# Latent attention by pairs of heads: 64-row score tiles and values stored split

## The chip, the cores and the metric

The kernel runs on one core of one Trainium2 chip. The metric is the device time of one execution in microseconds (us); the time of a kernel is the median of several executions. A core has five engines that run side by side, each with its own queue of instructions in a fixed order: TensorE (PE, matrix products; PEld is its loading of weights), VectorE (DVE), ScalarE (ACT), GpSimd (POOL) and SyncE (SP), which here only issues transfers (DMA). They work on an on-chip memory of 128 partitions (SBUF). Matrix products go into a small second memory of eight banks (PSUM), from which VectorE and ScalarE fetch them.

## The reference

The model is a trunk of two layers over 1024 tokens of width 1024, all in 32-bit floats. Layer 0 is differential attention, layer 1 is latent attention; a gated MLP with a short causal convolution follows each. Only layer 1's attention changes:

```python
def mla_attention(h, w_in, q_norm_g, kv_norm_g, w_uq, w_ukv, w_o, cos, sin):
    proj = h @ w_in                                            # 384 + 256 + 32 columns
    c_q = rms_norm(proj[..., :384], q_norm_g)
    c_kv = rms_norm(proj[..., 384:640], kv_norm_g)
    k_pe = apply_rope(proj[..., 640:], cos, sin)               # one rotary key for all heads
    q = (c_q @ w_uq).reshape(b, s, 16, 64 + 32)
    q_nope, q_pe = q[..., :64], apply_rope(q[..., 64:], cos, sin)
    kv = (c_kv @ w_ukv).reshape(b, s, 16, 64 + 64)
    k_nope, v = kv[..., :64], kv[..., 64:]
    # for each block of 128 queries
    sc = (einsum(q_nope, k_nope) + einsum(q_pe, k_pe)) * 96 ** -0.5
    p = masked_softmax(sc, chunk_mask)                         # key chunk (64) <= query chunk
    return einsum(p, v).reshape(b, s, 1024) @ w_o
```

There are 16 heads. A head's query and key have 64 plain columns and 32 rotary ones; the 32 rotary columns of the key are shared by all heads.

## The kernel before

**Precision.** A 32-bit operand x is held as a high part (x rounded to a format that TensorE takes at full speed, `hi`, L124) and a low part (x minus the high part, `lo`, L130). A product is three matmuls: high x low, high x high, low x high (`mm3`, L117 to L122). So L120, L121 and L122 are the lines of nearly every product, and L128 and L131 those of nearly every split.

**Stages of layer 1.** `mla_input` (L1540) makes the latents, token block by token block, transposes them, and makes the values (`values`, L1603), which go to DRAM (`v_d`) as plain floats. `mla_heads` (L1674) then works on 16 heads. Its projections are "units" of one half (512 tokens) each, written as generators that issue their matmuls, yield, and then empty the accumulator:

- `q_unit` (L1708), one for each head and half: 3 products of 3 matmuls. The weights have 128 columns a head: 64 plain, 32 rotary and the same 32 with their halves swapped, so that the rotation is one multiply by a table (L1720), after which 128 rows stand in one tile: plain, cosine part, sine part. High and low part follow.
- `k_unit` (L1724), one for a pair of heads and half: 2 products of 3 matmuls, 128 columns for two heads. It is emptied in two 64-row pieces into the key tiles of the two heads.
- The rotary key is rotated once and copied into rows 64 to 127 of four key tiles (`rotary`, `share`).
- `fetch_v`, `split_v` load a pair's values from `v_d` and split them.

**Steps.** The attention of a head is four steps. Step p has query blocks 2p and 2p+1 (of 128 queries each); block i has (i+1) x 128 keys. `MlaStep.scores` (L2005) makes one block's scores with three matmuls of 128 rows for each 512 keys into one score buffer S, masks the corner (L2017), takes the negated row maximum (L2018), and the exponential with its sum (L2019). `weigh` takes the reciprocal (L2025) and scales the row on GpSimd (L150). `turn` (L255) transposes the probabilities into banks "b" (L264) and splits them; `product` (L2028) multiplies with the split values into bank "u" (L2039, L2040), and adds the two halves of the result (L2042, L2043).

There are two S buffers of two banks each, three banks "b", shared by units and transposes, and one bank "u". `steps` (L293) is the program order: scores of this step's first block, a unit, the transposes of the step before, scores of the second block, units, the product of the step before. A scheduler reorders this by its own estimate of times: what is ready and stands first in program order goes first; an engine's order is then fixed. (In layer 0's attention the order is written out by hand; its scores, L1884, are already pairs of 64-row matmuls.) The steps of a head come in the order 1, 0, 3, 2. Strings such as `QUERIES_LOW` choose the engine of each split.

## Time and profile before

| | |
|---|---|
| time, median of 3 | 2373.07 us (2372.19 to 2373.26) |
| profiled execution: time, span | 2372.74 us, 2370.9 us |
| granted TensorE clock | 0.999 |
| busy share of PE, DVE, ACT, POOL | 99%, 81%, 53%, 25% |
| attention of layer 1: first to last masking (L2017) | 1289.7 to 1627.0 us of the span |

The span goes from the first to the last instruction. In a timeline row stand start, duration, engine, line, operation, the tile written and the tiles read, and the shape; brackets give the idle time before it and what ended it. In a row of groups the count is followed by the busy time, the mean of one in ns, and the engine's idle time before them with what ended it. Matmuls are pipelined, so their durations overlap.

### The profile page before, as it was taken

Reading aid. Unit: us, or ns where it says so; the run is one execution under the profiler, and the core shown is the slowest. Engines: PE = TensorE matmul, PEld = TensorE weight load, DVE = VectorE, ACT = ScalarE, POOL = GpSimd, SP = SyncE. Lnnn points to the kernel's source line nnn. Section 1 sums busy time; section 2 is a strip of 40 time slices with the busy share of each in tenths; the row PEclk is TensorE's granted clock in tenths of the full one; section 3 lists DMA queues with packets and bytes.
Section 4 is the critical chain, followed back from the end, with each engine's and each line's share of the span. In section 5 each row is a group of like instructions: output and inputs, shape, how many; then the busy total and the mean of one; then the engine's idle time right before and its main releaser. Section 6 shows DMA issues by size and latency. Waiting matters only on the chain.

```text
span 2370.9 us, 32976 instructions
## 1 busy us (share of the span) xinstructions
PE 2345.3 (99%) x12146; PEld 1976.2 (83%) x12146; DVE 1919.9 (81%) x3170; ACT 1259.6 (53%) x2315; POOL 583.5 (25%) x465
## 2 busy tenths in 40 slices
PE   9999999999999999999999999999999999999998
PEld 7888888788888888888898889988888888888886
DVE  6777878858888888999865888886588888889997
ACT  5666666745444444354444777775454444443444
POOL 4545444323000000000133666673420000000001
PEclk9999999999999999999999999999999999999999
DMA  3111111332222222652221211133322222227502
GB/s 148 40 36 36 49 37 54 111 134 94 89 80 81 80 89 80 234 174 86 84 99 56 72 33 39 41 98 110 114 79 88 80 80 83 87 80 284 178 1 80
DMA packets 95667, 213.42 MB, mean 90 GB/s; under 512 B 8713, under 2 KB 33937, under 8 KB 95505
## 3 DMA queue, kind: packets, MB, share of 16 engines
q1 hardware_dynamic: 86304, 183.51, 23.5%
q10 hardware_dynamic: 9200, 27.80, 3.2%
q8 instruction: 96, 1.57, 0.3%
q14 instruction: 67, 0.54, 0.1%
HBM read 158.85 MB, written 52.43 MB: 89 GB/s over the span
## 4 chain that ended last, share of the span: by engine, by line
PE 91%; DVE 5%; DMA 1%; ACT 1%; issue 1%; POOL 0%; POOLq 0%; DVEq 0%; SPq 0%; ACTq 0%
PE S L122 14%; PE S L120 14%; PE S L121 14%; PE b L120 9%; PE b L122 8%; PE b L121 8%; PE u L120 5%; PE u L122 5%; PE u L121 4%; PE S L1884 3%; PE b L264 2%; PE u L2040 1%; PE b L1930 1%; PE u L2039 1%; DVE s L131 1%
## 5 line engine op out<-in xcount | busy, mean ns | idle before, releaser
L168 POOL TENSOR_TENSOR st<-st,mhalf 128x1 f32<-128x1 f32 x56 | 35.3, 632 | 1296.1 <-DVE st L165 1287.4
L120 PE MATMUL S<-s,u 128*128 128x512 f32 (+1 forms) x800 | 301.8, 377 | 0.2 <-ACT u L1110 0.2
L122 PE MATMUL S<-s,u 128*128 128x512 f32 (+1 forms) x800 | 301.2, 376 | 0.1
L121 PE MATMUL S<-s,u 128*128 128x512 f32 (+1 forms) x800 | 301.0, 376 | 0.0
L128 ACT CAST u<-h 128x512 fp32r<-128x512 f32 (+1 forms) x194 | 115.8, 619 | 267.1 <-DVE h L1031 262.8
L120 PE MATMUL b<-s,u 128*128 128x512 f32 x588 | 230.8, 393 | 1.1 <-DVE u L131 0.4
L122 PE MATMUL b<-s,u 128*128 128x512 f32 x588 | 229.1, 390 | 0.0
L121 PE MATMUL b<-s,u 128*128 128x512 f32 x588 | 229.0, 389 | 0.0
L1088 DVE SCALAR_TENSOR_TENSOR u<-u,conv,u 128x1023 f32<-128x1023 f32 (+1 forms) x176 | 225.1, 1279 | 0.8 <-ACT u L1084 0.7
L150 POOL TENSOR_TENSOR u<-u,st 128x512 f32<-128x512 f32 (+7 forms) x160 | 173.1, 1090 | 161.1 <-DVE st L2025 107.3
L128 ACT CAST s<-u 128x512 fp32r<-128x512 f32 (+3 forms) x229 | 144.2, 663 | 100.2 <-PE u L122 28.7
L128 ACT CAST u<-b 128x512 fp32r<-128x512 f32 (+1 forms) x256 | 134.9, 547 | 92.1 <-PE b L1930 57.7
L131 DVE TENSOR_TENSOR u<-b,u 128x512 fp32r<-128x512 f32 (+1 forms) x256 | 158.6, 631 | 23.9 <-ACT u L128 22.8
L120 PEld LDWEIGHTS S<-s,u 128*128 128x128 f32 x800 | 150.6, 188 | 27.9 <-ACT u L1110 0.5
L122 PEld LDWEIGHTS S<-s,u 128*128 128x128 f32 x800 | 150.6, 188 | 27.8 <-DVE u L131 0.3
L121 PEld LDWEIGHTS S<-s,u 128*128 128x128 f32 x800 | 150.6, 188 | 27.4
L120 PE MATMUL u<-s,s 128*128 128x512 f32 (+1 forms) x408 | 165.1, 405 | 1.1 <-DVE s L131 0.9
L122 PE MATMUL u<-s,s 128*128 128x512 f32 (+1 forms) x408 | 158.3, 388 | 0.0
L121 PE MATMUL u<-s,s 128*128 128x512 f32 (+1 forms) x408 | 157.6, 386 | 0.0
L131 DVE TENSOR_TENSOR s<-u,s 128x512 fp32r<-128x512 f32 (+2 forms) x205 | 140.8, 721 | 15.0 <-ACT s L128 14.7
L1091 ACT ACTIVATE u<-u 128x1024 f32<-128x1024 f32 x44 | 46.7, 1062 | 187.4 <-DVE u L1088 187.4
L131 DVE TENSOR_TENSOR u<-h,u 128x512 fp32r<-128x512 f32 x171 | 118.1, 691 | 32.4 <-ACT u L128 31.5
(294 smaller groups left out, 6389.6 us busy)
## 6 DMA issues: line engine op xcount, KB each, us to landing
u<-in_ffn_up SPq DMA_DIRECT2D x88, 512.0 KB, 3.9
g_d<-u ACTq DMA_DIRECT2D x44, 512.0 KB, 2.6
u<-in_ffn_down SPq DMA_DIRECT2D x66, 256.0 KB, 4.7
u<-g_d SPq DMA_DIRECT2D x62, 256.0 KB, 4.1
s<-in_da_wqkv SPq DMA_DIRECT2D x23, 512.0 KB, 3.3
x_d<-u SPq DMA_DIRECT2D x16, 512.0 KB, 2.6
s<-x_d SPq DMA_DIRECT2D x8, 1024.0 KB, 10.5
s<-g_d SPq DMA_DIRECT2D x18, 256.0 KB, 5.3
```

The lines of the kernel that those rows point to most:

```text
L120: mm(out, lh, rl, start=first, stop=False, skip_group_check=onto)
L121: mm(out, lh, rh, start=False, stop=False, skip_group_check=onto)
L122: mm(out, ll, rh, start=False, stop=last, skip_group_check=onto)
L128: self.nc.scalar.copy(out, src)
L131: (eng or self.nc.vector).tensor_sub(out, src, hi.bitcast(F32))
L150: self.nc.gpsimd.tensor_mul(x, x, s.to_broadcast(list(x.shape)))
L168: nc.gpsimd.tensor_tensor(r, s, self.mhalf, ALU.pow)
L264: self.nc.tensor.transpose(ps[:, j * P : (j + 1) * P], probs[t][:, k : k + P], self.ident)
L1088: nc.vector.scalar_tensor_tensor(t[half][:, back:], u[half][:, : S - back], w, t[half][:, back:], ALU.mult, ALU.add)
L1091: nc.scalar.activation(t[0], t[0], AF.Silu)
L1884: nc.tensor.matmul(sc[c][:, b : b + m], q[rows, qp, qs], kt[rows, kp, :m], start=x == 0, stop=x == 2)
L1930: k.nc.tensor.transpose(ps[:, j * P : (j + 1) * P], self.e[t][0][:, c : c + P], k.ident)
```

## The change

Two heads are worked on together.

- The plain 64 query columns of two heads share one tile of 128 rows, as the keys do: `q_unit` and `k_unit` run once for each pair and half. The query tile is scaled and split straight from its accumulator (ScalarE multiplies, VectorE subtracts).
- The rotary columns of four heads (2 pairs) make one more unit, `r_unit`, for every second pair: 3 products of 3 matmuls, then a rotation in four passes (`rope`, L244: VectorE shuffles and multiplies, GpSimd multiplies and adds), two high parts on ScalarE and four low parts of 32 rows on VectorE. The tile has high and low part of a head's 32 rotary rows one below the other, 64 rows a head.
- The rotary key is one tile of 128 rows that holds it four times, with high and low part. The copies into key tiles are gone.
- Scores are five terms for each 512 keys: q low x k high, q high x k low, rotary x key low, rotary x key high, q high x k high. Each term is two matmuls of 64 rows, one for each head.
- A step has both heads. In steps 0 and 1 (up to 512 keys) both heads share one S; mask and maximum are one instruction for both. In steps 2 and 3 each head takes an S of its own, so a block takes both.
- The values are split when they are made, and stored split (twice the bytes); a load of values takes 1024 KB and needs no split.
- Transposes and products stay as they were, head by head; the sum of the products is done for both heads at once in a bank "u" of 512 columns.
- The steps of a pair come in the order 1, 3, 0, 2 (the first pair 1, 0, 3, 2, the last 1, 3, 2, 0). Units of the next pair stand in the second and the fourth step. The tables of engines are gone: every split's high part is on ScalarE; low parts are on VectorE, those of the weights and of the rotary key on GpSimd.

```diff
-    def steps(self, attend, units, prepare, n, apart=False):
+    def steps(self, attend, units, prepare, n):
...
                 now.scores(0)
...
+            self.run(u, 1)
             if before:
-                before.turn()
-            self.run(alone)
+                before.turn(0)
             if now:
                 now.weigh(0)
+            self.run(u, 2)
+            if now:
                 now.scores(1)
+            if before:
+                before.product(0)
+                before.turn(1)
             self.run(u)
-            if before:
-                before.product()
             if now:
                 now.weigh(1)
-            if t >= 2:
-                steps[t - 2].finish()
+            if before:
+                before.product(1)
...
         def values(i):
...
-                nc.scalar.copy(vs[:, b : b + 512], y)
-            nc.sync.dma_start(v_d[:, :, i].rearrange("h p e -> p h e"), vs.rearrange("p (h e) -> p h e", e=P))
+                vs = self.raw([P, D], F32R)
+                v = vs.rearrange("p (h a e) -> p h a e", a=2, e=64)
+                y = y.rearrange("p (h e) -> p h e", e=64)
+                self.hi(v[:, :, 0, :], y)
+                self.lo(v[:, :, 1, :], y, v[:, :, 0, :])
+                p = b // P
+                nc.sync.dma_start(v_d[p : p + 4, :, i].rearrange("h p e -> p h e"), vs.bitcast(F32).rearrange("p (h e) -> p h e", e=256))
...
-        v_ring, q_ring, t_ring = self.ring("s13", "s4"), self.ring("s1", "s11", "s5", "s9"), self.ring("h10", "h11", "h8")
-        k_places, kT = ["s0", "s10", "s12", "s8"], []
+        v_ring, k_ring, q_ring, r_ring = self.ring("s13", "s4"), self.ring("s1", "s12"), self.ring("s11", "s5"), self.ring("s10", "s8")
+        t_ring = self.ring("h10", "h11", "h8")
...
-            P=self.ring("u12", "u6", "u7", "u8", "u9"), pT=self.ring("u0", "u1", "u10", "u11"), o=self.ring("h4", "h5", "h6", "h7"),
+            P=self.ring("u12", "u6", "u7", "u8", "u9", lambda: piece(0), lambda: piece(1)), pT=self.ring("u0", "u1", "u10", "u11"), o=self.ring("h4", "h5", "h6", "h7"),
...
-            t = t_ring([P, 512])
-            nc.vector.tensor_mul(t, acc, cs[:, s])
-            self.hi(q[:, 0, s], t, eng(self.QUERIES[2 * h + half]))
-            self.lo(q[:, 1, s], t, q[:, 0, s], eng(self.QUERIES_LOW[2 * h + half]))
+            nc.scalar.mul(q[:, 0, s], acc, MLA_SCALE)
+            nc.vector.scalar_tensor_tensor(q[:, 1, s], acc, MLA_SCALE, q[:, 0, s].bitcast(F32), ALU.mult, ALU.subtract)
...
+        def r_unit(p, half):
+            if half == 0:
+                t = r_ring([P, 2, S], F32R)
+                pairs[p]["t"] = t
+                for x in range(2):
+                    pairs[p + x]["r"] = t[:, x, :]
+            t = pairs[p]["t"]
+            acc = project(p, 640, 3, cT.q, half)
+            yield
+            s = slice(half * 512, (half + 1) * 512)
+            r = self.rope(t_ring, acc, *tables(half), MLA_ROPE // 2)
+            for x in range(2):
+                self.hi(t[:, x, s], r)
+                for c in range(2):
+                    src, dst = (slice(64 * c + 32 * y, 64 * c + 32 * y + 32) for y in (x, 1 - x))
+                    self.lo(t[dst, x, s], r[src], t[src, x, s], self.RLOW(nc, p, x, c))   # nc.vector
+
+        def pair_units(p, *halves):
+            out = []
+            for half in halves:
+                if p < count:
+                    if p % 2 == 0:
+                        out.append(r_unit(p, half))
+                    out += [k_unit(p, half), q_unit(p, half)]
+            return out
...
         def units(t):
-            p, u = divmod(t, 8)
+            p, u = divmod(t, 4)
             if t == 0:
-                return [u() for u in pair_units(0)[1::2]]
+                return pair_units(0, 1)
+            at = (2, 3) if p == 0 else (1, 3)
+            return pair_units(p + 1, at.index(u)) if u in at else []
...
+            p, u = divmod(t, 4)
+            order = (1, 0, 3, 2) if p == 0 else (1, 3, 2, 0) if p + 1 == count else (1, 3, 0, 2)
+            return MlaStep(self, R, p, order[u], pairs[p], key, V, o_d)
...
     def scores(self, j):
...
+        if self.one:                                   # steps 0 and 1
+            both = k.big().rearrange("p (c n) -> p c n", c=2)[:, :, :n]
+            sc = [both[:, c, :] for c in range(2)]
+        else:
+            sc = [k.big()[:, :n] for _ in range(2)]
         for b, m in blocks(n):
-            k.mm3(sc[:, b : b + m], q[:, 0, qs], q[:, 1, qs], kt[:, 0, b : b + m], kt[:, 1, b : b + m], True, True)
-        nc.vector.memset(sc[0:64, n - 64 : n], NEG)
-        nc.vector.tensor_reduce(nm, sc, axis=AX.X, op=ALU.max, negate=True)
-        nc.scalar.activation(e, sc, AF.Exp, bias=nm, accum_out=l)
+            s = slice(b, b + m)
+            terms = [(q[:, 1, qs], kt[:, 0, s]), (q[:, 0, qs], kt[:, 1, s]), (r[:, qs], key[:, 1, s]), (r[:, qs], key[:, 0, s]), (q[:, 0, qs], kt[:, 0, s])]
+            for x, (lhs, rhs) in enumerate(terms):
+                for c in range(2):
+                    rows = slice(64 * c, 64 * c + 64)
+                    nc.tensor.matmul(sc[c][:, s], lhs[rows], rhs[rows], start=x == 0, stop=x == 4)
...
+        if self.one:
+            nc.vector.memset(both[0:64, :, n - 64 : n], NEG)
+            nc.vector.tensor_reduce(nm, both, axis=AX.X, op=ALU.max, negate=True)
+        for c in range(2):
+            if not self.one:
+                nc.vector.memset(sc[c][0:64, n - 64 : n], NEG)
+                nc.vector.tensor_reduce(nm[:, c : c + 1], sc[c], axis=AX.X, op=ALU.max, negate=True)
+            nc.scalar.activation(e[c], sc[c], AF.Exp, bias=nm[:, c : c + 1], accum_out=l[:, c : c + 1])
```

More of the change, by code (lines that the diff above doesn't have):

```diff
@@ L291, in run @@
                 n -= 1
-    def steps(self, attend, units, prepare, n, apart=False):
-        steps = []
-        for t in range(n + 2):
-            now = before = None
+    def steps(self, attend, units, prepare, n):
+        now = None
+        for t in range(n + 1):
+            before, now = now, None
             u = []
@@ L1633, in mla_input @@
             if i == NT - 2:
[L1634 to L1635 removed]
+                heads.first(0, 1)
             if i == NT - 1:
[L1637 removed]
+                heads.first(2)
             if i < NT:
@@ L1686, in mla_heads, with fetch_sine, tables, rotary @@
         )
-        eng = lambda x: {"S": None, "V": nc.vector, "P": nc.gpsimd}[x]
+        def fetch_sine():
+            for half in range(2):
+                sine.append(self.at(f"h{12 + half}", [P, 512]))
+                nc.sync.dma_start(sine[half], a["rope"][:, 1, half * 512 : (half + 1) * 512])
+        def tables(half):
+            return cosine[:, half * 512 : (half + 1) * 512], sine[half]
+        def rotary():
+            if not key:
+                key.append(self.at("s0", [P, 2, S], F32R))
+            return key[0]
@@ new lines, in fetch_v, with project, q_unit @@
+            nc.sync.dma_start(V[p].bitcast(F32).rearrange("p k h a e -> p k (h a e)"), v_d[p])
+        def project(p, off, n, latent, half):
+            acc = self.bank()
+            for k in range(n):
+                wh, wl = (w[:, off + k * P : off + (k + 1) * P] for w in W[p])
+                self.mm3(acc, wh, wl, latent(0, half, k), latent(1, half, k), k == 0, k == n - 1)
+            return acc
+        def q_unit(p, half):
+            if half == 0:
+                pairs[p]["q"] = q_ring([P, 2, S], F32R)
+            q = pairs[p]["q"]
+            acc = project(p, 0, 3, cT.q, half)
@@ L1747, in first @@
         def first(*which):
-            self.run([pair_units(0)[x]() for x in which])
+            self.run([(k_unit, r_unit, q_unit)[x](0, 0) for x in which])
         def own(i, y):
@@ L1813, in rest, with RLOW @@
             self.run(work)
-        return SimpleNamespace(early=early, first=first, own=own, rotary=rotary, share=share, rest=rest)
+        return SimpleNamespace(early=early, first=first, own=own, rotary=rotary, tables=tables, fetch_sine=fetch_sine, rest=rest)
+    @staticmethod
+    def RLOW(nc, p, x, c):
+        return nc.vector
 class Step:
```

221 lines of the change are left out of this document (82 added, 139 removed).

## The prediction, made before the changed kernel was run

> **What bounds the kernel now.** I read the page's first part and its chain first, then the busy time of the latent attention by stretches, then TensorE's timeline of one head, and last the groups by line.
>
> ```profile
> PE 2345.3 (99%) x12146; PEld 1976.2 (83%) x12146; DVE 1919.9 (81%) x3170; ACT 1259.6 (53%) x2315; POOL 583.5 (25%) x465
> ...
> PE 91%; DVE 5%; DMA 1%; ACT 1%; issue 1%; POOL 0%; POOLq 0%; DVEq 0%; SPq 0%; ACTq 0%
> ```
>
> ```profile
> 1200.00:1290.00 90.00, 90.00 (x563) 85.55 (x562) 42.12 (x97) 44.54 (x120) 24.60 (x29) 1.00 0.21 66
> 1310.00:1592.00 282.00, 279.17 (x1797) 249.28 (x1796) 233.66 (x566) 216.00 (x470) 187.80 (x147) 1.00 0.16 49
> 1592.00:1627.00 35.00, 33.82 (x250) 31.04 (x248) 30.11 (x77) 28.61 (x65) 24.80 (x20) 1.00 0.33 101
> ```
>
> Columns after the times: the stretch, then PE, PEld, DVE, ACT, POOL, granted clock, DMA share. The change lies in these stretches alone: latents and values, the attention while projections of the next pair are left to do, and the last pair, which has none. TensorE idles 2.8 us of 282 in the middle one, at full clock, while VectorE has 83%, ScalarE 77%, GpSimd 67%. So TensorE's own time counts, as long as the rest can keep it fed.
>
> The timeline of TensorE in one head; matmuls overlap, so I read the distance of starts, not the durations:
>
> ```profile
> 1410.96 0.95 PE L264 MATMUL b<-ident,u 128*128 128x128 f32 x7
> 1411.66 0.48 PE L120 MATMUL S<-s,s 128*128 128x512 f32 x1
> ...
> 1435.26 0.39 PE L120 MATMUL b<-s,u 128*128 128x512 f32 x1
> ...
> 1436.62 0.28 PE L2039 MATMUL u<-u,s 128*128 128x256 f32 x1
> 1436.74 0.28 PE L2040 MATMUL u<-u,s 128*128 128x256 f32 x1
> ```
>
> A transpose is 0.10 us (0.70 for 7), a matmul of 512 columns 0.227 (six from 1435.26 to 1436.62), one of 256 is 0.12; I take 0.12 as the least for 128 columns too.
>
> **The change part by part.**
>
> Projections. Before, a pair of heads issues 4 query units of 9 matmuls and 2 key units of 6: 48. After: 2 plain query units (18), 2 key units (12), and for every second pair 2 rotary units (18, or 9 a pair): 39. 8 x 9 = 72 fewer, x 0.227 = 16.4 us off TensorE, at full price, since it is the engine that is busy.
>
> Scores. Before, a head runs 3 terms over 4608 columns in all (128 to 1024): 3 x 4608/512 x 0.227 = 6.13, and the narrow 128-column pieces of the first and the fifth block take 0.12 instead of 0.057 each: 6 x 0.06 = 0.4. 6.5 a head, 13.1 a pair. After, 5 terms, each as two 64-row matmuls. The differential attention already does this, and its timeline has the price:
>
> ```profile
> 307.86 0.60 PE L585 MATMUL b<-ident,h 128*128 128x128 f32 x4
> 308.38 1.66 PE L1884 MATMUL S<-u,u 64*128 64x512 f32 x12
> 309.97 0.50 PE L120 MATMUL u<-s,s 128*128 128x512 f32 x1
> 310.30 0.40 PE L121 MATMUL u<-s,s 128*128 128x512 f32 x1
> 310.54 0.39 PE L122 MATMUL u<-s,s 128*128 128x512 f32 x1
> ```
>
> Twelve matmuls of 512 columns pass in 1.59 us, so two row halves do run side by side. But going in and out costs: from 308.38 to 310.54 there are 6 pairs and 2 full matmuls, 8 x 0.227 = 1.82, in 2.16: 0.34 lost; on the way in, 4 transposes take 0.52 where 0.40 would do: about 0.1 more. 0.4 us for each entry and exit. A pair after: 5 x 4608/512 x 0.227 = 10.2, narrow pieces 10 x 0.06 = 0.6, 8 calls x 0.4 = 3.2: 14.0. So scores cost 0.9 more a pair, 7 us in all, where the columns alone (6.13 x 2 against 10.2) promise 2 us less a pair.
>
> The Trainium skill, page TensorEngine Tiling (Array Packing), section Theoretical Speedup, gives up to 2x for a contraction of 64 rows; by that alone, without the 0.4 a call, scores would go from 13.1 to 10.8 and TensorE would save 16.4 + 8 x 2.3 = 35 us. The same page's Key Properties say that changing the tiling mode drains TensorE; the 0.34 above agrees, so I go by the row.
>
> Transposes (72 a pair) and value products (80 a pair) stay the same in number and shape; the key's transpose of 32 rows becomes 128, still one of 0.10.
>
> Side engines. Removed and added in the attention, from these groups (mean ns after the comma):
>
> ```profile
> L131 POOL TENSOR_TENSOR s<-h,s 128x512 fp32r<-128x512 f32 x30 | 38.8, 1294 | 6.9 <-ACT s L128 6.3
> L150 POOL TENSOR_TENSOR u<-u,st 128x1024 f32<-128x1024 f32 x16 | 30.3, 1894 | 5.1 <-DVE st L2025 5.1
> L150 POOL TENSOR_TENSOR u<-u,st 128x896 f32<-128x896 f32 x16 | 26.9, 1681 | 55.3 <-DVE st L2025 55.0 <-PE S L122 0.3
> L150 POOL TENSOR_TENSOR u<-u,st 128x768 f32<-128x768 f32 x16 | 23.5, 1467 | 5.5 <-DVE st L2025 3.9 <-PE b L264 0.9
> ```
>
> ```profile
> L131 DVE TENSOR_TENSOR s<-b,s 64x512 fp32r<-64x512 f32 x32 | 22.0, 686 | 3.6 <-ACT s L128 3.1
> L1720 DVE TENSOR_TENSOR h<-b,u 128x512 f32<-128x512 f32 x32 | 21.9, 686 | 13.4 <-PE b L122 12.8
> L2018 DVE TENSOR_REDUCE st<-S 128x1 f32<-128x1024 f32 x16 | 19.6, 1223 | 1.2
> L2025 DVE RECIPROCAL st<-st 128x1 f32<-128x1 f32 x128 | 19.5, 152 | 7.9 <-ACT u L2019 7.6
> L2018 DVE TENSOR_REDUCE st<-S 128x1 f32<-128x896 f32 x16 | 17.5, 1092 | 0.6
> L2018 DVE TENSOR_REDUCE st<-S 128x1 f32<-128x768 f32 x16 | 15.1, 947 | 0.7
> L2017 DVE MEMSET S<- 64x64 f32 x128 | 14.3, 112 | 10.4 <-PE S L122 8.9
> L2018 DVE TENSOR_REDUCE st<-S 128x1 f32<-128x640 f32 x16 | 13.0, 811 | 0.2
> ```
>
> ```profile
> L2019 ACT ACTIVATE u<-S,st 128x1024 f32<-128x1024 f32 x16 | 17.9, 1117 | 6.5 <-DVE st L2018 4.1 <-DVE st L2025 2.0
> L2019 ACT ACTIVATE u<-S,st 128x896 f32<-128x896 f32 x16 | 16.2, 1016 | 15.9 <-DVE S L2017 10.7 <-DVE st L2018 5.2
> L128 ACT CAST s<-u 128x1024 fp32r<-128x1024 f32 x14 | 14.7, 1053 | 6.1 <-DMA u<-in_mla_w_o 4.3 <-PE b L122 1.4 <-DMA u<-v_d 0.4
> L2019 ACT ACTIVATE u<-S,st 128x768 f32<-128x768 f32 x16 | 14.5, 905 | 5.5 <-DVE st L2018 3.7 <-DVE st L2025 1.7
> L2019 ACT ACTIVATE u<-S,st 128x640 f32<-128x640 f32 x16 | 12.8, 800 | 2.5 <-POOL s L131 1.4 <-DVE st L2018 0.9
> ```
>
> VectorE: the multiply L1720 (32 x 0.69) goes; 32 low parts of keys become 16 of the same length, as 128 rows take no longer than 64; 16 low parts of queries come (16 x 0.69); 64 reciprocals go (9.7); 8 rotary units add six passes each, at 0.69 by the L1720 row (33). Net -22 - 11 + 11 - 10 + 33 = about 0. GpSimd loses 38.8 and gains two multiplies a rotary unit (16 x 1.3 = 21). ScalarE loses the V splits (7 x 1.05) and about half of its query and key copies. All of this lies beside TensorE; I price it at nothing. V is now split before it is stored: 16 low parts (11 us) move to VectorE in the stretch 1200:1290, where it has 42 of 90 busy, and the bytes through v_d double, on a DMA share of 0.16 to 0.21 and a pair ahead of use; behind them on SP's queue stand the weight fetches, a pair ahead too. If that cover failed, one wait of some microseconds at the first pair would show.
>
> The wait that is added. There are two score buffers S. Before, one row block of one head takes one S, so the other holds the next block. After, blocks over 512 columns take both, one for each head, and the next block can start only when both row maxima and both exponentials are done, two of each in line:
>
> ```profile
> 1435.42 0.55 DVE L131 TENSOR_TENSOR u<-b,u 128x384 fp32r<-128x384 f32 x1
> 1435.97 0.11 DVE L2017 MEMSET S<- 64x64 f32 x1
> 1436.18 1.23 DVE L2018 TENSOR_REDUCE st<-S 128x1 f32<-128x1024 f32 x1
> ```
>
> ```profile
> 1437.50 1.12 ACT L2019 ACTIVATE u<-S,st 128x1024 f32<-128x1024 f32 x1
> ```
>
> Here the scores ended when the next matmul came (1435.26), and the exponential ended at 1438.62: 3.4 us, against 0.11 + 1.22 + 1.12 = 2.45 of work. The 0.9 is queueing, a subtraction ahead of the memset among it; I take it for every such hold. Now each gap of the new order (blocks 384/512, 896/1024, 128/256, 640/768), against the TensorE work that the program puts into it:
>
> - After 896: two memsets and maxima 2.4, the last exponential 1.0, queue 0.9: 4.3. TensorE has 7 transposes 0.7, a key unit 1.4, a query unit 2.0: 4.1, with a rotary unit 6.1.
> - After 1024, until the transposes of this step can start: 2.7 + 1.1 + reciprocal 0.15 + GpSimd 1.9 + 0.9 = 6.7. TensorE has products and transposes of the 384/512 step 2.6, then two small score calls 2.0: 4.6. Short by 2.1.
> - After 640: 1.85 + 0.8 + 0.9 = 3.55, against 3.7 or 5.7.
> - After 768, until its transposes: 2.1 + 0.9 + 0.15 + 1.5 + 0.9 = 5.5, against 1.3 + the calls of 384 and 512, 2.8: 4.1. Short by 1.4.
>
> The scheduler can pull units forward, so surplus fills shortage. Batches with a rotary unit (3 of 7) have 1.8 + 2.1 spare, and the 3.5 is made good. The 4 without have 0.2 missing more, 0.15 spare: 3.55 each, 14.2 in all. The last pair has no units: after 1024 only 2 us of the 6.7 is covered, after 896 3.3 of 4.3; about 6 us idle, against 1.2 now (35.00 - 33.82): 5 more.
>
> The sum: -16.4 + 7 + 14.2 + 5 = +9.8. The profiled execution took 2372.74 (span 2370.9 and 1.8 around it), 0.3 under the median of 2373.07, so 2383.
>
> Bounds of that wait: with no queueing the shortages are 1.2 and 0.5 and the spare about 1.7, so nothing is left but some 3 us at the last pair: -6, 2366. With twice the queueing 7.2 for each batch without a rotary unit, 3 with: 38, and 7 at the end: +36, 2408. I take 0.9 because it is what this very hold shows. This is the likeliest case's own range.
>
> **The rivals.**
>
> TensorE stays fed. The scheduler orders by its own reckoning and has seven probability tiles and free projection units; GpSimd, with 39 us of subtractions gone, delivers earlier. The last bound holds then, or a little better, as the start of the attention loses the copies of the key's rotary rows: -16.4 + 7 + 0 to 3 = -6 to -10, about 2364. For it: 2.8 us idle now, though VectorE is 83% busy. Against it: now only one S of two is held. It decides as soon as stalls stay under 5 us over eight pairs.
>
> The halves come apart. S of the first head comes free one exponential (0.8 to 1.1) before that of the second, or earlier. If the first head's terms are issued at once, they run alone and their partners alone after them: up to 5 x 0.227 = 1.1 us a call, four calls a pair, 36 us, of which the idle time above would cover half: 9.8 + 18 = +28, 2400. That two halves never run side by side is excluded by 308.38.
>
> It cancels: stalls of 5 to 14 us eat about the 9 that TensorE saves; 2368 to 2377.
>
> The page's section PSUM Bottleneck says that tiling speeds TensorE but not the emptying of PSUM; no sum here uses it, and it speaks for the waits.
>
> **How the numbers follow.** S held too long (slower) 0.39; TensorE fed (faster) 0.32; halves apart (slower) 0.09; it cancels 0.20. A change under 0.2% (4.7 us) can't be told from none. So slower 0.48, same 0.20, faster 0.32; predicted 2383. The range goes from the fed case with a little to spare, 2360, to past the halves apart, 2402.
>
> **What would show it.** Rows of the projection accumulators: 72 matmuls fewer. The score line: starts of two halves 0.00 apart, pairs 0.23, calls with 0.4 around them. In the stretch of the attention, TensorE idle well over 4 us, its score matmuls released by the exponential's line, its transposes by GpSimd's multiply or VectorE. GpSimd's busy share falls. I am wrong if TensorE's idle time there stays at 3 us (then faster), or if first-half matmuls run in rows of five without partners (then slower still), or if VectorE's six rotary passes push the maxima back and TensorE waits for them.

## The result, and the profile after

The changed kernel takes 2483.97 us (median of 4 runs, 2459.64 to 2494.19) against 2373.16 for the kernel before on the same chip: a ratio of 1.0452, 95% interval 1.0375 to 1.0530. It is slower, as forecast, but by 111 us where 10 were forecast, far outside the range. Its runs differ by 35 us because the granted clock does: span times clock is 2434 to 2438 in every one of them (2485.8 x 0.979 and 2457.8 x 0.992 are two), against 2370.9 x 0.999 = 2368.5 before. The rest of this part is the execution with a span of 2485.8.

The page's first part looks almost as before, and hides everything:

```profile
PE 2452.6 (99%) x12458; PEld 2029.2 (82%) x12458; DVE 1929.0 (78%) x3039; ACT 1231.7 (50%) x2258; POOL 546.7 (22%) x445
...
PEclk9999999999999999999999888989999999999999
...
PE 93%; DVE 4%; DMA 1%; ACT 1%; issue 1%; POOL 0%; SPq 0%; POOLq 0%; DVEq 0%; ACTq 0%
```

TensorE is busy 99% in both kernels and holds more of the chain (93% for 91%). Only the clock row has eights. The stretches say where (the columns are those of the first part of the prediction; the granted clock is the third value from the end):

```profile
1200.00:1290.00 90.00, 90.00 (x565) 85.21 (x565) 49.84 (x109) 41.90 (x117) 25.52 (x30) 1.00 0.29 96
1310.00:1701.00 391.00, 378.81 (x2058) 300.49 (x2058) 239.35 (x446) 191.93 (x416) 150.52 (x125) 0.88 0.14 45
1701.00:1765.00 64.00, 64.00 (x402) 54.10 (x400) 39.65 (x69) 36.03 (x71) 26.70 (x22) 1.00 0.34 104
```

In the first stretch, latents and values, TensorE works throughout, as before. The middle one (until the last projection) grew from 282 to 391 us, the rest, until the last value product, from 54 (1592 to 1646.4) to 64. VectorE, ScalarE and GpSimd are less busy there than before: none of them became the bound by its sum. TensorE's waits there are few:

```profile
PE b L264 <- DVE s L1719: 11.0, 3, 5.3
PE S L2029 <- ACT u L2040: 0.6, 2, 0.5
...
```

So the time is in TensorE's own instructions. I add up the distances of their starts by line, from 1290 us to the last value product, idle time apart; at half clock, half of a distance goes to the line and half to a column of its own. (The matmuls of the output projection in S are counted as "other": 67 before, 16 us, and 83 after, 19 us.) All rows are us:

| kernel | scores | transposes | products | other | idle | half clock | sum |
|---|---|---|---|---|---|---|---|
| before | 113.4 | 56.0 | 76.0 | 105.6 | 5.3 | 0 | 356 |
| after | 168.5 | 70.2 | 82.7 | 94.5 | 12.6 | 46.4 | 475 |
| difference | +55.1 | +14.2 | +6.7 | -11.1 | +7.3 | +46.4 | +118.6 |

The span grew by 114.9, so this stretch is all of it (the rest gave back 4). Two items carry it: the scores, and the half clock. (Without the 16 more matmuls of the output projection, "other" falls by 14.6.)

**The scores.** Two heads' halves side by side were to be the point of the change. The timeline of TensorE shows one head, then the other:

```profile
1475.94 2.31 PE L2029 MATMUL S<-s,s 64*128 64x512 f32 x10
1478.18 1.10 PE L264 MATMUL b<-ident,u 128*128 128x128 f32 x8
1479.37 2.30 PE L2029 MATMUL S<-s,s 64*128 64x512 f32 x10
1481.59 0.39 PE L2058 MATMUL u<-u,s 128*128 128x256 f32 x1
```

Ten matmuls of 64 rows take 2.3 us, 0.23 each, and half of the array has nothing to do. Only about 155 of the 480 pairs start together.

**The half clock.** The clock falls four times, for 10.2, 41.0, 20.5 and 23.9 us:

```profile
1331.50:1341.80 10.30, 10.30 (x37) 8.46 (x36) 4.87 (x10) 4.02 (x8) 4.35 (x4) 0.50 0.00 0
...
1406.60:1447.60 41.00, 37.97 (x113) 28.64 (x114) 16.90 (x29) 11.87 (x23) 7.79 (x6) 0.50 0.15 45
...
1532.90:1553.40 20.50, 20.50 (x68) 16.30 (x66) 8.32 (x15) 6.74 (x14) 6.08 (x5) 0.50 0.08 27
...
1645.50:1669.40 23.90, 23.90 (x74) 18.44 (x73) 9.14 (x17) 7.89 (x16) 6.26 (x6) 0.50 0.03 9
```

The last three begin during TensorE's three waits for L1719 or within 0.4 us of their end. VectorE's queue at the first of them, then TensorE's:

```profile
1403.07 5.79 DVE L131 TENSOR_TENSOR s<-h,s 32x512 fp32r<-32x512 f32 x4 [0.34 <-ACT s L128]
1408.89 0.69 DVE L1719 SCALAR_TENSOR_TENSOR s<-b,s 128x512 fp32r<-128x512 f32 x1
```

```profile
1403.40 0.96 PE L2029 MATMUL S<-s,s 64*128 64x512 f32 x6
1409.63 0.48 PE L264 MATMUL b<-ident,u 128*128 128x128 f32 x1 [5.27 <-DVE s L1719]
```

The four rotary low parts of 32 rows take 5.8 us; the query's low part stands behind them in VectorE's queue, holds a bank, and the transposes wait for the bank. It is the same at 1528 (4.96 us of them, 3.97 of waiting) and 1643 (2.77 and 1.77).

### The profile page after: what moved, and what is told of

Same layout as the page of the kernel before. It is cut to its first block, busy times and chain, and to the rows that moved or that the text cites. A ratio compares the mean times of both kernels' runs of the same rounds, so it can differ in the third digit from the quotient of the medians.

```text
span 2485.8 us, 33241 instructions
## 1 busy us (share of the span) xinstructions
PE 2452.6 (99%) x12458; PEld 2029.2 (82%) x12458; DVE 1929.0 (78%) x3039; ACT 1231.7 (50%) x2258; POOL 546.7 (22%) x445
## 4 chain that ended last, share of the span: by engine, by line
PE 93%; DVE 4%; DMA 1%; ACT 1%; issue 1%; POOL 0%; SPq 0%; POOLq 0%; DVEq 0%; ACTq 0%
PE S L122 12%; PE S L120 12%; PE S L121 12%; PE b L120 8%; PE b L122 8%; PE b L121 8%; PE S L2029 7%; PE u L120 5%; PE u L122 4%; PE u L121 4%; PE b L264 3%; PE S L1882 2%; PE u L2058 2%; PE u L2059 2%; DVE s L131 1%; PE b L1928 1%
## 5 line engine op out<-in xcount | busy, mean ns | idle before, releaser
L128 ACT CAST u<-h 128x512 fp32r<-128x512 f32 x192 | 114.5, 619 | 264.9 <-DVE h L1027 262.8
L128 ACT CAST u<-b 128x384 fp32r<-128x384 f32 (+1 forms) x264 | 140.0, 549 | 177.8 <-PE b L264 73.3
L120 PE MATMUL b<-s,u 128*128 128x512 f32 x572 | 226.9, 397 | 0.0
L121 PE MATMUL b<-s,u 128*128 128x512 f32 x572 | 224.9, 393 | 0.0
L122 PE MATMUL b<-s,u 128*128 128x512 f32 x572 | 224.8, 393 | 0.0
L131 DVE TENSOR_TENSOR u<-b,u 128x384 fp32r<-128x384 f32 (+1 forms) x264 | 164.1, 635 | 51.0 <-ACT u L128 50.1
L2029 PE MATMUL S<-s,s 64*128 64x512 f32 (+3 forms) x960 | 200.5, 384 | 1.0 <-ACT u L2040 0.6
L128 ACT CAST s<-u 128x512 fp32r<-128x512 f32 (+2 forms) x221 | 135.7, 649 | 100.6 <-PE u L122 28.0
L2029 PEld LDWEIGHTS S<-s,s 64*128 64x128 f32 x960 | 141.7, 200 | 46.5 <-issue 19.3
L150 POOL TENSOR_TENSOR u<-u,st 128x128 f32<-128x128 f32 (+7 forms) x129 | 133.1, 1048 | 191.6 <-DVE st L2044 138.9
```

Of the source, the lines that this page charges most:

```text
L120: mm(out, lh, rl, start=first, stop=False, skip_group_check=onto)
L121: mm(out, lh, rh, start=False, stop=False, skip_group_check=onto)
L122: mm(out, ll, rh, start=False, stop=last, skip_group_check=onto)
L128: self.nc.scalar.copy(out, src)
L131: (eng or self.nc.vector).tensor_sub(out, src, hi.bitcast(F32))
L150: self.nc.gpsimd.tensor_mul(x, x, s.to_broadcast(list(x.shape)))
```

## The experiments

Each kernel's time stands against the kernel before, run on the same chip beside it (2372.1 to 2372.8). The first four are edits of the changed kernel.

**1. Both halves side by side (tied).** A full-row matmul of 128 columns into the first head's S (overwritten afterwards) and a fixed order of the score matmuls make both halves wait until both buffers are free:

```diff
+            if b == 0 and not self.one:
+                nc.tensor.matmul(sc[0][:, 0:128], q[:, 0, qs], kt[:, 0, 0:128], start=True, stop=True)
...
-                for c in range(2):
+                for c in (1, 0):
...
+                    k.tc.keep_in_program_order(mm)
```

> Only the order of the score matmuls changes: a full-row matmul of 128 columns into the first head's buffer (overwritten afterwards) and ordering edges make both halves wait until both buffers are free, then go side by side. Theory A, halves issued apart are the main cost: in the changed kernel's profile the score line takes 157.6 us of starts at full clock and 45.5 at half, 180 at full clock in all, against 112 worked out for pairs side by side. So about 68 us come back, score line near 115 us; with the clock as it was, 2484 - 68 = 2416. Theory B, the clock falls because TensorE runs dry behind VectorE's rotary subtractions (idle gaps of 5.3, 4.0 and 1.8 us): the clock stays at 0.98 to 0.99, so 2410 to 2425. Theory C, the clock falls because a half alone uses half of the array: the clock goes back to 0.998, 2484 - 68 - 45 = about 2370. Theory D, my forecast (the two score buffers held too long): the waits for the buffers take the place of the halves alone, and 2400 or more stays even at full clock.

Measured: 2440.94 (ratio 1.0287, 1.0271 to 1.0302).

**2. Rotary low parts on GpSimd (rot_pool).** `RLOW` returns `nc.gpsimd`.

> Only the 32 low parts of 32 rows of the rotary units move from VectorE to GpSimd. Theory B (those subtractions, 0.7 to 2.7 us each, block VectorE's queue, the banks of the projections stay full, TensorE runs dry, and the clock drops): the idle gaps of 2 us and more go, the clock is back at 0.997 or more, and the four runs' spread of 35 us goes with it: 2435 to 2440. Theory C (halves alone drop the clock): the clock stays at 0.98 and the time at 2470 to 2490. Theory A says nothing of it: the score line stays at 180 us at full clock.

Measured: 2441.13 (1.0290, 1.0275 to 1.0306).

**3. Both of these (tied_pool).**

> Both edits. If A and B are the two causes and independent: 2484 - 68 - 45 = about 2370, at full clock, 0 to 10 us under or over the kernel before. Theory D, the score buffers: TensorE idle 20 us or more in the attention at full clock, 2385 to 2400.

Measured: 2425.23 (1.0223, 1.0208 to 1.0238).

**4. Halves apart throughout (apart).** The loop over the two heads stands outside the loop over the five terms.

> All matmuls of the first head stand before those of the second in program order, in every block, the small ones too. Theory A: a pair's scores then cost 2 x 10.8 + 3.2 = 24.8 us, 198 in all at full clock, 18 more than the changed kernel; 2490 to 2510. Theory C: the granted clock falls well below 0.97, and the time goes over 2520. Theory B: the clock stays in the range of the changed kernel, 0.977 to 0.992.

Measured: 2478.65 (1.0450, 1.0433 to 1.0468); the profiled run has a span of 2466.2.

The same sums for the four; the scores of 1 and 3 include 7 to 8 us of the added matmul:

| kernel | scores | transposes | products | other | idle | half clock | sum |
|---|---|---|---|---|---|---|---|
| 1 tied | 112.2 | 69.1 | 82.8 | 94.2 | 53.2 | 12.8 | 424 |
| 2 rot_pool | 167.3 | 70.7 | 83.4 | 95.0 | 6.3 | 6.7 | 429 |
| 3 both | 111.9 | 69.2 | 82.6 | 94.0 | 41.5 | 12.6 | 412 |
| 4 apart | 178.7 | 71.0 | 83.8 | 95.5 | 10.8 | 15.4 | 455 |

What follows. The fourth shows that the changed kernel runs nearly apart already (168.5 of 178.7); it stays under the 2490 to 2510 expected, as its score lines rose by 10 us, not 18, and its half clock is shorter. The first shows that side by side does what the layer-0 row promised, though its time lies above the 2370 to 2425 of theories A to C; 20 matmuls now take the time of ten, here in the third kernel:

```profile
1449.38 2.30 PE L2031 MATMUL S<-s,s 64*128 64x512 f32 x20
1451.61 0.38 PE L2062 MATMUL u<-u,s 128*128 128x256 f32 x1
```

But of the 56 us saved in the score lines 41 come back as idle time: of the 53.2 us, 24 are waits for S, which slow matmuls had filled while the halves ran apart, and 25 are waits for VectorE's lines. The third kernel, with both edits, misses both of its expectations (2370, and 2385 to 2400): its idle time is 41.5 us, where 20 or more were expected, and 12.6 us of half clock are left. The second takes 43 us off by moving these subtractions (four for each rotary unit; a group row of the changed kernel, by shape, in the stretch), nearly all of it half clock: 46.4 to 6.7, as theory B expected, and its four runs lie within 2.6 us where those of the changed kernel differ by 35.

```profile
L131 DVE TENSOR_TENSOR s<-h,s 32x512 fp32r<-32x512 f32 x28 | 24.8, 887 | 3.8 <-ACT s L128 3.3
```

So the three long drops came from the waits behind them. Halves apart do not pull the clock down by themselves: the second kernel has as many of them (167.3 us of score lines), and the granted clock of its four runs is 0.996 or 0.997; the fourth has even more, and 0.987 to 0.993, where the changed kernel has 0.977 to 0.992.

**5 to 8. The hold of the score buffers, from kernel 3 (hold_short, hold_long, side_long, side_short).** Shorter: no mask and maximum for the second head in blocks over 512 columns. Longer: that maximum twice. Beside it: one more maximum of the same length, from a query tile, behind it. And less load beside it: without the addition of the low half of the products.

```diff
+            bare = c == 1 and not self.one
-            if not self.one:
+            if c == 0 and not self.one:
...
-            nc.scalar.activation(e[c], sc[c], AF.Exp, bias=nm[:, c : c + 1], accum_out=l[:, c : c + 1])
+            nc.scalar.activation(e[c], sc[c], AF.Exp, bias=0.0 if bare else nm[:, c : c + 1], scale=0.0 if bare else 1.0, accum_out=l[:, c : c + 1])
```

```diff
+        if not self.one:
+            nc.vector.tensor_reduce(k.stat(), q[:, 0, :n].bitcast(F32), axis=AX.X, op=ALU.max, negate=True)
```

> The kernel with both halves side by side and the rotary low parts on GpSimd (2425), but without the mask and the maximum of the second head in the blocks over 512 columns (its exponential takes a scale and a bias of zero): 32 blocks keep both score buffers about 1.13 us less each, 36 us in all. Theory 'the score buffers are held too long': most of the 41 us of TensorE's idle time there and of the 27 us at half clock is paid for by these holds; the idle time falls to 10 to 20 and the time to 2385 to 2405. Rival 'the copies and subtractions of the transposed probabilities set the pace': the idle time stays within 8 us of 41 and the time at 2417 to 2428.

> The same kernel (2425) with the second head's maximum taken twice in the blocks over 512 columns: each hold 1.02 us longer, 32 x 1.02 = 33 us. Theory 'held too long': nearly all of it is paid, idle time about 70, 2450 to 2465, more if the half clock grows with it. Rival 'VectorE's load as such': the same rise as with the load beside the hold (below). Rival 'the probabilities' chain': 2425 to 2435.

> The same kernel (2425) with one more maximum of the same length on VectorE behind the second head's maximum, read from a query tile: VectorE has the same 33 us more as with the maximum taken twice, but the second head's exponential does not wait for it, so the buffers are not held longer. Theory 'held too long': clearly less than the longer hold costs, 2428 to 2442 (the reciprocal and the next subtractions still come a microsecond later). Rival 'VectorE's load as such': the same as with the longer hold, 2450 to 2465.

> The kernel with both halves side by side and the rotary low parts on GpSimd (2425), without the addition of the low half of the value products (32 x 0.675 = 21.6 us less on VectorE; that half is left out of the output), which holds no score buffer. Theory 'VectorE's queue as such, in whose order the low parts of the probabilities stand, counts beside the hold': the 33 us more beside the hold cost 35, so 22 less gain 10 to 22: 2403 to 2415. Rival 'only the hold counts below this load': 2418 to 2427.

Measured: shorter hold 2396.01, longer hold 2478.20, more beside it 2460.29, less beside it 2436.26 (kernel 3: 2425.23). TensorE's waits, kernel 3 first, then the shorter hold, then the load beside it (us, times, longest):

```profile
PE S L2031 <- ACT u L2044: 9.5, 10, 1.6
PE b L264 <- DVE u L131: 7.0, 9, 1.4
PE S L2027 <- ACT u L2044: 6.9, 7, 1.8
PE u L2062 <- DVE u L131: 6.2, 6, 2.7
PE S L2027 <- ACT s L2044: 3.6, 3, 2.3
PE S L2031 <- ACT s L2044: 2.4, 3, 1.3
...
```

```profile
PE b L264 <- DVE u L131: 5.6, 9, 0.9
PE u L2063 <- DVE u L131: 5.1, 10, 1.5
...
PE S L2031 <- ACT u L2045: 1.7, 2, 0.9
PE S L2031 <- ACT s L2045: 1.5, 2, 1.3
...
```

```profile
PE u L2064 <- DVE u L131: 25.6, 14, 3.8
PE S L2031 <- ACT u L2044: 9.2, 8, 1.6
PE b L264 <- DVE u L131: 6.3, 9, 1.4
PE S L2027 <- ACT u L2044: 4.4, 6, 1.6
PE S L2031 <- ACT s L2044: 3.2, 3, 1.3
PE S L2027 <- ACT s L2044: 3.1, 2, 1.7
...
```

What follows. The shorter hold takes the waits for S from 22.4 us to about 4, the idle time from 41.5 to 20.9 and the half clock from 12.6 to 3.4: 29 us, as the hold theory expected. It also takes those maxima off VectorE's queue, so this run alone does not part the hold from the load. The load beside the hold leaves the waits for S where they were (20 us). Its price (35 us, not the 3 to 17 expected) is 16 us more idle time and 18 more of half clock, and the idle time comes from another wait, the value products' for the low parts of the probabilities, 6.2 to 25.6: these stand behind the extra maximum in VectorE's queue. So the load met the rival's range, yet in another place than the longer hold, which came out above both (2478, with 33 us of waits for S, 65.5 of idle time and 41.0 of half clock): VectorE's order costs beside the hold. The last kernel is a miss of both: 22 us less work on VectorE, by count, came out 11 us slower. Its idle time (44.7) is spread like that of kernel 3. After this edit TensorE's instructions stand in another order from 1317 us on, and I read the 11 us as the worth of such an order here, which no run shows by itself; differences of that size between these kernels are not explained by their edits.

**9, 10. One part alone: the projections, and V stored split (hybrid, vsplit).** The steps and scores of one head at a time are those of before (the query rows of a score tile are 96: 64 plain, 32 rotary); projections are the change's. The rotated query rows reach the heads' tiles through DRAM:

```diff
+            x = self.raw([P, 2, 512], F32R)
+            self.hi(x[:, 0, :], r)
+            self.lo(x[:, 1, :], r, x[:, 0, :], nc.gpsimd)
+            nc.sync.dma_start(r_d[p // 2][:, :, s], x.bitcast(F32))
...
-            k.mm3(sc[:, b : b + m], q[:, 0, qs], q[:, 1, qs], kt[:, 0, b : b + m], kt[:, 1, b : b + m], True, True)
+            k.mm3(sc[:, b : b + m], q[:ROWS, 0, qs], q[:ROWS, 1, qs], kt[:ROWS, 0, b : b + m], kt[:ROWS, 1, b : b + m], True, True)
```

The second kernel is the one before with V stored split and nothing else.

> One part alone: the projections of the change (a unit for the plain columns of two heads, one for the rotary columns of four, 39 matmuls a pair for 48) and V stored split, with the kernel before's steps and its scores of one head as full-row matmuls (96 rows of contraction; the rotated query rows reach them through DRAM). Theory 'all the loss lies in the form of the scores and of the steps': 72 fewer matmuls x 0.227 = 16.4 us less on TensorE, idle time in the attention as before (5 us), no stretch at half clock: 2356 (2348 to 2364). Rival 'the rotary unit's passes and the values' low parts on VectorE starve TensorE': they are still there (six passes for each of 8 units, 33 us of VectorE), so idle time and half clock come back: 2372 to 2395.

> One part alone: the kernel before, with V split before it is stored and its two parts fetched straight into the ring, and nothing else changed. Theory 'this part is hidden': the values' low parts on VectorE (16 x 0.69 = 11 us) lie where it has 42 of 90 us busy, and ScalarE and GpSimd lose their split of V: 2370 to 2375. Rival 'it costs a wait at the first pair': 2376 to 2382. What the projections alone lost against their 16 us would then be this part's or not.

Measured: projections 2387.69 (1.0063, 1.0048 to 1.0078), V stored split 2375.53 (1.0013, 1.0004 to 1.0022). V stored split costs 3 us, no more than two orders of the same work differ by (experiments 12 and 13: 3.7), so the projections alone lose some 12 where they should have gained 16. Their matmuls did go (other: 105.6 to 88.5), but idle time rose to 20.1 and half clock to 9.6.

**11. The same, with its two visible waits mended (hybrid2).** Rotary units ahead of key and query units; one scaled copy a head out of the bank, low parts of the queries on GpSimd.

> The projections alone (2387.69, with 20 us of idle time and 20 us at half clock in the attention, where the kernel before has 5 and 0), mended at the two places that its trace names: the rotary units of a group of four are issued ahead of its key and query units, so that the rotated rows are through DRAM in time (6.2 us of waits on them), and the query columns leave their bank by one scaled copy for each head, on VectorE and ScalarE, with the low parts on GpSimd as before the change (5.0 us of transposes waiting for VectorE's low parts of the queries). Theory 'these waits, and the half clock that follows them, are all that hides the 16 us': 2355 to 2366. Rival 'the projections leave TensorE no filler, so that idle time comes back at other places': 2370 to 2388.

Measured: 2402.17 (1.0124, 1.0110 to 1.0138), worse, outside both expectations. One wait for the rotated rows remains (6.8 us), and new ones for S (8.3) and for low parts of probabilities (7.4) took the place of the mended ones.

**12 to 14. Is the attention of before bound by TensorE (less_terms, less_units, more_terms)?** The kernel before with 72 projection matmuls left out, single terms in one kernel and whole contraction steps in the other, or 72 added. The first:

```diff
-                self.mm3(acc, wh, wl, cT.q(0, half, k), cT.q(1, half, k), k == 0, k == 2)
+                (self.mm3 if k == 0 else self.mm2)(acc, wh, wl, cT.q(0, half, k), cT.q(1, half, k), k == 0, k == 2)
...
-                self.mm3(acc, wh, wl, cT.kv(0, half, k), cT.kv(1, half, k), k == 0, k == 1)
+                (self.mm2 if k == 0 and half == 0 else self.mm3)(acc, wh, wl, cT.kv(0, half, k), cT.kv(1, half, k), k == 0, k == 1)
```

> The kernel before, with 72 projection matmuls left out (one low term each of two of the three contraction steps of every query unit, one of every first key unit: 9 a pair; the projections lose those terms), and nothing else changed: no engine but TensorE has less to do. Theory 'TensorE bounds the attention, as the prediction took it': 72 x 0.227 = 16.4 less, 2352 to 2360. Rival 'the projections are filler for a chain over VectorE and ScalarE': idle time and half clock take the place of the matmuls, 2366 to 2376.

> The kernel before, with 72 projection matmuls left out in another way (the query units of every second head sum over one or two of their three contraction steps: 6 and 3 a pair), and nothing else changed. Both theories expect the same as of the run above (2352 to 2360, or 2366 to 2376); the difference of the two is the scatter that a new order of the same work brings, expected under 4 us.

> The kernel before, with 72 projection matmuls added (the same places, each term taken twice; the projections gain those terms), and nothing else changed. Theory 'bound by TensorE': 16.4 more, 2386 to 2392. Rival 'filler': 2373 to 2382, since some of it lies in idle time. The theory 'TensorE' allows at most 5 us in idle time, which is all there is.

Measured: 2379.34 (1.0030, 1.0018 to 1.0042), 2375.68 (1.0013, 1.0003 to 1.0022), and with 72 added 2395.47 (1.0097, 1.0081 to 1.0114). This is the run that decides about the forecast's first term: 16 us of TensorE's work less, and the kernel is 3 to 7 us slower, in two ways of doing it. From 1290 us on, before and then the kernel with single terms left out:

```profile
1290.00:1646.40 356.40, 351.12 (x2242) 312.22 (x2240) 292.01 (x690) 265.61 (x575) 228.05 (x179) 1.00 0.22 65
```

```profile
1290.00:1653.30 363.30, 342.72 (x2167) 302.68 (x2165) 294.87 (x686) 261.66 (x570) 226.46 (x179) 0.99 0.21 63
```

TensorE's other matmuls fell from 105.6 to 89.0 us; idle time rose from 5.3 to 20.6, half clock took 3.4, and the transposes and products came 6 us slower. One of the waits, and what VectorE did:

```profile
1447.04 0.50 PE L126 MATMUL b<-s,u 128*128 128x512 f32 x1 [0.98 <-DVE s L137]
```

```profile
1445.37 0.89 DVE L2024 TENSOR_REDUCE st<-S 128x1 f32<-128x768 f32 x1
1446.29 0.69 DVE L137 TENSOR_TENSOR s<-b,s 64x512 fp32r<-64x512 f32 x1
```

A projection wants a bank; the bank is emptied by a subtraction that stands behind a row maximum. In the kernel with whole steps left out (17.1 us of idle time) the longest waits are for S, 8.2 us, and for low parts of probabilities, 6.6. Adding 72 matmuls cost 23 us, above the 16.4 of their own, and the idle time grew with them: a miss for both theories at the upper end.

**15 to 18. Is it VectorE (vec_free, vec_free_less, hybrid_free, tied_free)?** The low parts of the transposed probabilities (99 of VectorE's 292 us) are left out, and the high part is multiplied twice, so TensorE's work stays: in the kernel before, in it with 72 matmuls left out, in kernel 9 and in kernel 3.

```diff
-            self.lo(l[:, :m], ps[:, :m], h[:, :m])
-            out.append((h, l))
+            out.append((h, h))
```

> The kernel before, without the low parts of the transposed probabilities (160 subtractions on VectorE, 98.6 of its 294 us in the attention); the value products read the high part twice instead, so TensorE has the same matmuls. Theory 'TensorE and VectorE's queue are in balance there': only the 5 us of idle time can be gained, 2365 to 2372. It is the base for the next run.

> The same, and 72 projection matmuls left out (single low terms spread over the units, as in the run that gave 2379). Theory 'VectorE's queue is the floor under TensorE's work': now the 16.4 us show at full price, 14 to 17 below the run above, 2349 to 2357. Rival 'the floor is ScalarE, GpSimd or the program's order': within 6 us of the run above.

> The change's projections with the scores and steps of before (2388), without the low parts of the transposed probabilities as above. Theory 'VectorE's queue': the idle time falls from 20 to the 6 us of waits for the rotated rows and a little more, and 2388 becomes 2352 to 2364. Rival: 2372 to 2386.

> The kernel with both halves side by side and the rotary low parts on GpSimd (2425), without the low parts of the transposed probabilities as above. Theory 'VectorE's queue': the waits on those low parts go (about 17 us) and so does most of the waiting for score buffers, whose maxima stand in the same queue; idle time 41 to about 12, half clock 27 to under 10: 2372 to 2392. Rival 'the hold as such, two maxima and two exponentials in line': the 22 us of waits for score buffers stay, 2395 to 2412.

Measured: 2374.53 (1.0010, 1.0000 to 1.0019), 2367.58 (0.9979, 0.9970 to 0.9989), 2384.96 and 2411.61. A third of VectorE's work there gone gains nothing by itself (not even the 5 us of idle time that were expected). With it gone, the 72 matmuls bring 7 us (2374.53 to 2367.58) where they brought none before: not the 14 to 17 of the theory "VectorE's queue is the floor", nor quite the rival's "within 6", and no more than twice the 3.7 us by which two orders of the same work differ. What TensorE then waits for is this:

```profile
PE S L126 <- ACT u L2024: 12.2, 11, 2.1
PE b L270 <- ACT u L134: 0.8, 2, 0.4
```

That is the hold of S again, by one head's maximum and exponential, at the start and at the end of the attention; between 1320 and 1564 us no wait over half a microsecond is left, where the run with VectorE's full load has a dozen for VectorE's lines. In the two forms of the change the relief gives 3 and 14 us, which is what the rivals expected: the holds stay (16 us of waits for S in the last kernel).

## Why the prediction was wrong

**The first term, "16.4 us off TensorE, at full price, since it is the engine that is busy", failed.** The matmuls went, as counted (other, at the same number of output projection matmuls: -14.6 after, -17.1 with the projections alone). But nothing of it was to be had: experiments 12 and 13 take the same matmuls out of the kernel before and gain nothing. 99% busy with 2.8 us idle in 282 was read as "TensorE sets the time". It meant that TensorE's work just covered the wait for S and for VectorE's queue; the projections were the filler. The page gave a hint that was passed over: VectorE had 83% and ScalarE 77% in the same stretch, each standing in a chain with waits.

**The price of the scores, +7, was mis-sized at both ends.** Before, the score lines take 113.4 us, where 13.1 a pair, 105 in all, was counted. Side by side they take 105.0 (without the added matmul), where 14.0 a pair, 112, was counted. So the lines themselves gain 8. But the entries and exits were priced inside the score calls alone, and the neighbours' lines grow too: transposes +13 and products +7 in experiment 1, part of it caused by the matmul added there. So the form costs up to 12 where 7 was said.

**"The halves come apart" was the rival that happened, at .09.** Its price, 36 us, took 1.1 a call; calls over 512 columns have two such blocks, and nearly all calls came apart: 63.5 us (168.5 - 105.0) of the 74 possible (178.7 - 105.0). That half of it would lie in idle time that the hold makes anyway was right, or low: taking the halves together gave back 41 of 56 in idle time.

**The likeliest case, S held too long, is there, but larger.** 14.2 and 5 us of shortages were forecast; with the halves together the idle time is 41.5 to 53.2, of which 22 to 24 in waits for S, against 5.3 before. The shorter hold of experiment 5 pays 29 us for 36 us less of holding. Why the forecast was low is argued, not shown: it let TensorE's surplus in one gap cover the shortage of another, and took VectorE's queue as 0.9 us in each, which the load beside the hold shows to grow.

**"All of this lies beside TensorE; I price it at nothing" failed for the rotary unit.** VectorE's sum did come out at about nothing (292.01 before, 293.47 after). But an average does not say what stands behind what: four subtractions in a row, 2.8 us even at the 0.69 of the row used, made the transposes wait 1.8, and at the two longer waits they took 5.0 and 5.8. This was named as what would make the prediction wrong, and priced at nothing; moving them off took 43 us away.

**The clock was not in the sum at all.** It is 46 us of the 119, in the execution shown.

**What held:** the count of the matmuls, VectorE's sum, V stored split near nothing, and a larger wait for S. The direction held too, but in part by luck: most of the loss, the halves apart and the half clock, was not in the sum.

**What stays open.** Which chain sets the floor of the kernel before is settled in part: VectorE's queue in the middle of the attention, since its relief takes every wait there away, and the hold of S at both ends; why the relief brings 7 us and not 16 is only partly covered by those 12 us of waits. No order of the pair form without these waits was found, and no kernel that computes everything came out under the one before. A third S buffer was not tried, since the eight banks are full.

## What to carry to other kernels

A busy share of 99% at full clock does not make an engine's every microsecond count: ask what the engine would do instead of the work that goes, and look for what the second engine's queue holds then. If that is a wait, the work was filler; a run that only leaves the work out tells it before anything is built. Two half-array matmuls are only worth it if the program makes them start together, since a scheduler that takes what is ready starts the first head's as soon as its own buffer is free, and tying them brings the wait for the second buffer into the open. And small instructions on a side engine are priced by what stands behind them in its queue.

## What the runs showed of the hardware

The clock falls to half in steps of 3.41 us (10.2, 20.5, 23.9 and 41.0 are 3, 6, 7 and 12 of them), and in the changed kernel it stays low for longer than the wait that began it: 41 us after one of 5.27 us, 23.9 after one of 1.77. The Trainium skill, page TensorE: Matmul & The Clock Gate, section What's actually happening, gives windows of 3413 ns and two values, half and full; the trace agrees with both. The section Why this matters for your kernels of that page of the Trainium skill asks only to avoid idle gaps over about 3 us; here the first drop, at 1331.5, follows 0.46 us of idle time, and the last 1.77, so the measurement is stricter. The length of a wait alone does not decide it: in experiment 1 waits of 1.97 and 2.12 us (until 1366.4 and 1452.2 us) were followed by no drop, one of 1.98 us (until 1654.2) by one 1.3 us later. What decides is not worked out here.

A subtraction of 32 x 512 on VectorE from one on-chip tile to another took 2.77 or 2.78 us for four in the five rotary units of the changed kernel with no GpSimd instruction beside them, and 3.33, 4.96 and 5.79 in the three with 1.4, 2.3 and 4.6 us of GpSimd work beside them; on GpSimd the four took 5.3 each time.
